# Two moves at the end of each group of a state-space stage: the last fill product ahead of x's transposes, the third chunk's exponents between the result's transposes

## The chip, the core and the metric

The kernel runs on one core of a Trainium2 chip. The core has TensorE (PE in the rows, its weight loads PEld), VectorE (DVE), ScalarE (ACT), GpSimd (POOL) and SyncE (SP, which issues most DMAs). Each engine works its own queue in order. The metric is device time in microseconds, the median of three runs.

## What is computed

Two transformer-like blocks for 512 tokens of width 1024, all in float32. The change touches the first block's state-space branch alone: eight groups of four heads (64 wide, state 128), two scan directions, four chunks of 128 tokens. Of the reference:

```python
xbc = jax.nn.silu(depthwise_conv(xbc, conv_w, conv_b))      # x, b and c of every group
decay = segsum_exp(a_dt)                                    # exp of differences, 128 x 128 per chunk and head
cb = jnp.einsum('bclgn,bcsgn->bcgls', c, b)
y_diag = jnp.einsum('bcgls,bcgrls,bcsgrp->bclgrp', cb, decay, xdt)
states = jnp.einsum('bclgn,bcgrl,bclgrp->bcgrpn', b, decay_states, xdt)
...
y_off = jnp.einsum('bclgn,bcgrpn,bcgrl->bclgrp', c, prev, jnp.exp(a_cs))
...
y = y_fwd + y_bwd + xs * d_skip.astype(jnp.float32).reshape(G, R, 1)
u = y * jax.nn.silu(z.astype(jnp.float32))                  # then a norm per group and the output product
```

## The kernel before, in words

Weights come in units of 1 MB. Each is loaded to a tile `raw`, cast by ACT to its high part `whi` (L140), and DVE makes the low part `wlo` (L141). A product is three products of high and low parts: L286 to L288 with channels on the partitions, L304 to L306 with tokens on them. All of them write the PSUM banks `psg`, of which there are two: a third product starts when the first one's bank has been read.

The loop over the groups runs from about 60 to 505 us. In the loop of group g the state-space work of g is mixed with the products for g + 1. What is issued, and in which order, is written out by hand in the string `GSEQ` (L29 to L31), a list of step names for the groups 0 to 6; group 7 has `LAST_GSEQ`. The names that matter here:

- `z0` to `z3`: the product for z, one for each tile of 128 tokens (L304 to L306). ACT copies each from its bank to `sz` (L630). The first use of a unit also casts the next unit in the stream.
- `f0` to `f7`: the fill, which is the next group's products. In most groups `f4` and `f5` are the two halves of x's first tile of channels, `f6` and `f7` the halves of its second one; for group 4 each of `f4` to `f7` is a whole tile, and `f6`, `f7` are the two of x. After the last half comes `conv_silu` (L587): ACT copies the bank to `cbuf` (L591) and scales it (L592), DVE adds four taps (L594), ACT takes the Silu (L595). L592 is the last reader of the bank.
- `xt0`, `xt1`: four transposes on PE of x's first and second tile (L600), copied by ACT to `xt` (L601). `xt1` is in the next group's loop, behind `z0 w0`.
- `e0` to `e3`: the next group's exponents for a chunk (`exponents`, L677). For each of the two directions one matmul into a bank `pse` (L685, two banks), one Exp on ACT (L687) into `e0` (two buffers) or `e1` (one buffer), one masking on POOL (L688); then one addition on POOL (L692) into `w` (four buffers).
- `w0` to `w3` (L697): cb times the exponents' sum. `cb` (L656). `st0` to `st2` (L667, from `xw`, L664): the states. `y0` to `y3`: the output; ACT ends each with a square and its sum (L724).
- `norm`: an inverse root on POOL (L343), four scalings on ACT (L729).
- `u0`, `u1`: four transposes on PE each (L734) into `pso` and `psy`; ACT makes `ua_h` of each (L337), DVE `ua_l` (L338).
- `rows`: two DMAs per direction for the next group's exponents, issued by POOL (L648, L650).

`GSEQ` isn't the queues' order. The program is built by a framework whose planner walks the traced instructions with the string's order as priority: when, by its own account of durations, an engine is free, it gives it the first instruction by priority whose inputs and buffers are there. So steps that wait are overtaken, and each engine's queue is then fixed. Which activation table ScalarE holds is settled on the finished queue: an `ACT_TABLE_LOAD` stands where Exp follows Silu or the other way round. Copies, scalings and squares go with either table.

Of the kernel before, what the change touches and what calls it, by code (L numbers as in the profile page):

```python
# [26 lines left out]
NF = 8  # L27
LAST_GSEQ = "z0 xt1 st0 w0 z1 st1 w1 z2 w2 st2 z3 w3 silu y0 k0 y1 y2 y3 norm k1 u0 k2 u1 k3"
GSEQ = """  # L29
z0 w0 xt1 st0 z1 w1 z2 z3 st1 silu st2 y0 f0 f1 y1 rows f2 f3 w2 e0 y2 e1 w3 f4 f5 bt y3 norm f6 e2 xt0 f7 u0 u1 cb e3  # L30
"""  # L31
SEQ = """v.0 v.1 v.2 v.3 p0 v.4 n0 v.5 v.6 v.7 c0 G u.0 L0.0 L0.1 L0.2 W0.0 u.1 W0.1 L0.3 p1 W0.2 n1 W0.3 u.2 u.3 f0 c1
L1.0 o.0 o.1 L1.1 W1.0 o.2 L1.2 L1.3 S o.3 p2 P0 W1.1 n2 W1.2 o.4 B0.0 x0 W1.3 o.5 f1 c2 B0.1 o.6 L2.0 L2.1 x1
# [1865 lines left out]
```

## Time and profile before

| what | value |
| --- | --- |
| median of 3 runs | 1914.93 us (1913.95 to 1914.96) |
| the profiled execution, its own time | 1915.58 us |
| its span, first to last instruction | 1913.8 us |
| PE busy | 1846.5 us, 96% |
| ACT, DVE, POOL busy | 937.4, 1142.9, 439.4 us |

The span is what the views below are cut from; 1.8 us of the execution's time lie around it. A row of a timeline gives the start, the length, the engine, the line, the operation, the tiles (out<-in) and how many instructions are merged; in brackets, how long the engine was idle before and what ended that. Rows that follow on one engine overlap a little, so a chain is read from start to start.

### The profile page before, as it was taken

The numbers are of one execution on the slowest core, as the hardware profiler recorded it, in microseconds if no ns is written. First come the engines' busy times: TensorE is split into PE (matmuls) and PEld (weight loads), VectorE is DVE, ScalarE is ACT, GpSimd is POOL, SyncE is SP. The second block draws the span as 40 slices with busy tenths as digits, with TensorE's granted clock in tenths as the row PEclk, the third lists the DMA queues.
The fourth block names the chain that finished last, engine by engine and source line by source line (L and its number), as shares of the span: only waits on it lengthen the run. The fifth ranks groups of instructions, "written<-read, shape, count | busy, mean of one in ns | idle before, by whom it ended". The sixth has DMA issues, their size and how long they took to land. (4 is left out here: it accounts for less than half of the span.)

```text
span 1913.8 us, 24517 instructions
## 1 busy us (share of the span) xinstructions
PE 1846.5 (96%) x9585; PEld 1525.0 (80%) x9585; DVE 1142.9 (60%) x1796; ACT 937.4 (49%) x1511; POOL 439.4 (23%) x498
## 2 busy tenths in 40 slices
PE   8899999999999999998999999989999999999998
PEld 7688888888887777887888888878877768888886
DVE  6767762666456554537233434567667785766768
ACT  6756672766335665345332313345443454444534
POOL 1454441443202321234011201231210330000000
PEclk9999999999999999999999999999999999999999
DMA  5222112221332222333333232322211232324211
GB/s 170 75 68 68 52 62 88 68 68 46 102 93 66 82 79 67 126 119 110 100 98 111 88 110 89 110 74 59 73 45 55 78 132 77 125 85 132 88 44 44
DMA packets 161186, 164.10 MB, mean 86 GB/s; under 512 B 8743, under 2 KB 148718, under 8 KB 161071
## 3 DMA queue, kind: packets, MB, share of 16 engines
q1 hardware_dynamic: 148858, 150.90, 25.0%
q10 hardware_dynamic: 9716, 10.02, 1.7%
q0 software_dynamic: 2496, 1.61, 0.4%
q8 instruction: 75, 1.23, 0.3%
q14 instruction: 41, 0.33, 0.1%
HBM read 158.26 MB, written 4.23 MB: 85 GB/s over the span
## 5 line engine op out<-in xcount | busy, mean ns | idle before, releaser
L141 DVE TENSOR_TENSOR wlo<-raw,whi 128x1024 fp32r<-128x1024 f32 (+3 forms) x253 | 321.4, 1286 | 223.5 <-ACT whi L140 219.3
L286 PE MATMUL psg<-hh,whi 128*128 128x512 f32 (+1 forms) x1016 | 404.2, 398 | 0.8 <-DVE hl L338 0.8
L287 PE MATMUL psg<-hl,whi 128*128 128x512 f32 (+1 forms) x1016 | 401.0, 395 | 0.0
L140 ACT CAST whi<-raw 128x1024 fp32r<-128x1024 f32 (+3 forms) x253 | 254.7, 1028 | 298.4 <-PE psg L287 255.0
L288 PE MATMUL psg<-hh,wlo 128*128 128x512 f32 (+1 forms) x1016 | 399.5, 393 | 0.0
L286 PEld LDWEIGHTS psg<-hh,whi 128*128 128x128 f32 (+1 forms) x1016 | 191.0, 188 | 40.3 <-issue 1.2
L288 PEld LDWEIGHTS psg<-hh,wlo 128*128 128x128 f32 (+1 forms) x1016 | 191.0, 188 | 39.8
L287 PEld LDWEIGHTS psg<-hl,whi 128*128 128x128 f32 (+1 forms) x1016 | 190.9, 188 | 38.2 <-DVE hl L335 0.4
L286 PE MATMUL psg<-ua_h,whi 128*128 128x512 f32 x544 | 216.3, 399 | 0.8 <-DVE xT L1585 0.5
L287 PE MATMUL psg<-ua_l,whi 128*128 128x512 f32 x544 | 213.8, 393 | 0.0
L288 PE MATMUL psg<-ua_h,wlo 128*128 128x512 f32 x544 | 212.7, 391 | 0.0
L304 PE MATMUL psg<-whi,hh 128*128 128x256 f32 x416 | 122.1, 294 | 10.1 <-ACT cacc L592 3.6
L286 PEld LDWEIGHTS psg<-ua_h,whi 128*128 128x128 f32 x544 | 102.0, 188 | 26.0 <-DVE xT L1585 2.4
L305 PE MATMUL psg<-wlo,hh 128*128 128x256 f32 x416 | 119.8, 288 | 1.0 <-DVE wlo L141 1.0
L306 PE MATMUL psg<-whi,hl 128*128 128x256 f32 x416 | 120.2, 289 | 0.0
L287 PEld LDWEIGHTS psg<-ua_l,whi 128*128 128x128 f32 x544 | 102.3, 188 | 21.7 <-issue 1.0
L288 PEld LDWEIGHTS psg<-ua_h,wlo 128*128 128x128 f32 x544 | 102.2, 188 | 20.8
L1187 POOL TENSOR_TENSOR fsq<-relu 128x512 f32<-128x512 f32 x32 | 40.5, 1267 | 243.5 <-ACT relu L1184 228.2
L1009 POOL TENSOR_TENSOR ssq<-ssq,sq 128x512 f32<-128x512 f32 x42 | 66.3, 1578 | 117.2 <-ACT sq L1008 115.9
L141 DVE TENSOR_TENSOR wlo<-quad,whi 128x1024 fp32r<-128x1024 f32 x56 | 66.9, 1222 | 43.0 <-ACT whi L140 43.0
L304 PEld LDWEIGHTS psg<-whi,hh 128*128 128x128 f32 x416 | 80.0, 192 | 15.7 <-ACT sz L630 5.1
L140 ACT CAST whi<-quad 128x1024 fp32r<-128x1024 f32 x56 | 57.0, 1049 | 70.0 <-PE psg L287 32.9
(628 smaller groups left out, 3547.7 us busy)
## 6 DMA issues: line engine op xcount, KB each, us to landing
raw<-in_w_in_dram SPq DMA_DIRECT2D x37, 1024.0 KB
raw<-in_w_mlp_in_dram SPq DMA_DIRECT2D x16, 1024.0 KB
raw<-in_w_mlp_out_dram SPq DMA_DIRECT2D x16, 1024.0 KB
raw<-in_w_ff_dram SPq DMA_DIRECT2D x16, 1024.0 KB
quad<-in_w_ff_dram SPq DMA_DIRECT2D x16, 1024.0 KB
raw<-in_w_in_dram SPq DMA_DIRECT2D x16, 512.0 KB
raw<-in_w_ssd_out_dram SPq DMA_DIRECT2D x8, 1024.0 KB
raw<-in_w_attn_out_dram SPq DMA_DIRECT2D x4, 1024.0 KB
```

The source lines that it names most:

```text
L140: A.copy(self.hi[sl], self.raw[sl])
L141: V.tensor_tensor(out=self.lo[sl], in0=self.raw[sl], in1=self.hi[sl].bitcast(F32), op=ALU.subtract)
L286: T.matmul(o, lhsT=u.hi[:, k, c:e], rhs=xh[k], start=k == 0, stop=False)
L287: T.matmul(o, lhsT=u.hi[:, k, c:e], rhs=xl[k], start=False, stop=False)
L288: T.matmul(o, lhsT=u.lo[:, k, c:e], rhs=xh[k], start=False, stop=k == u.kt - 1)
L304: T.matmul(o, lhsT=xh[k][:, tk], rhs=u.hi[:, k, 0 : u.n], start=k == 0, stop=False)
L305: T.matmul(o, lhsT=xh[k][:, tk], rhs=u.lo[:, k, 0 : u.n], start=False, stop=False)
L306: T.matmul(o, lhsT=xl[k][:, tk], rhs=u.hi[:, k, 0 : u.n], start=False, stop=k == u.kt - 1)
L1009: G.tensor_tensor(out=self.t, in0=self.t, in1=q, op=ALU.add)
L1187: G.tensor_tensor(out=f, in0=r, in1=r, op=ALU.mult)
```

## The change

One line of `GSEQ`. `f7` comes ahead of `xt0`, and `e2` comes behind `u0` and ahead of `u1`. So `e2` is passed by `f7`, `xt0` and `u0`. Nothing is added or removed, and `LAST_GSEQ` stays.

```diff
 GSEQ = """
-z0 w0 xt1 st0 z1 w1 z2 z3 st1 silu st2 y0 f0 f1 y1 rows f2 f3 w2 e0 y2 e1 w3 f4 f5 bt y3 norm f6 e2 xt0 f7 u0 u1 cb e3
+z0 w0 xt1 st0 z1 w1 z2 z3 st1 silu st2 y0 f0 f1 y1 rows f2 f3 w2 e0 y2 e1 w3 f4 f5 bt y3 norm f6 f7 xt0 u0 e2 u1 cb e3
 """
```

## Rows read from the trace of the kernel before

**Rows 1.** The page: its head and the busy time of each engine.
```profile
span 1913.8 us, 24517 instructions
...
PE 1846.5 (96%) x9585; PEld 1525.0 (80%) x9585; DVE 1142.9 (60%) x1796; ACT 937.4 (49%) x1511; POOL 439.4 (23%) x498
```

**Rows 2.** Busy time in stretches: the change-over from group 2 to group 3, then one whole period. Columns: stretch, its length, busy us (and instructions) of each engine, granted PE clock, DMA share, GB/s.
```profile
206.00:229.00 23.00, 20.12 (x135) 17.57 (x133) 15.81 (x21) 18.56 (x31) 14.36 (x20) 1.00 0.22 64
212.00:264.00 52.00, 49.24 (x284) 42.29 (x284) 36.16 (x51) 33.64 (x56) 24.67 (x35) 1.00 0.20 63
```

**Rows 3.** PE in order of time, 206 to 229 us: `e2`, `cb`, and every start that came after a wait.
```profile
206.90 0.62 PE L685 MATMUL pse<-rh,lh 128*128 128x512 f32 x2
...
210.07 1.05 PE L656 MATMUL psc<-cT,bT 128*128 128x128 f32 x8
...
213.01 0.66 PE L600 MATMUL pst<-ident,cacc 128*128 128x128 f32 x4 [1.19 <-ACT cacc L595]
...
218.07 0.39 PE L304 MATMUL psg<-whi,hh 128*128 128x256 f32 x1 [0.58 <-ACT cacc L592]
...
222.35 0.39 PE L304 MATMUL psg<-whi,hh 128*128 128x256 f32 x1 [0.39 <-ACT sz L630]
...
226.17 0.66 PE L600 MATMUL pst<-ident,cacc 128*128 128x128 f32 x4 [0.20 <-ACT cacc L595]
...
228.48 0.70 PE L667 MATMUL pso<-xw,bt 128*128 128x256 f32 x2 [0.46 <-DVE xw L664]
```

**Rows 4.** ACT in order of time, 208 to 226 us.
```profile
208.83 0.19 ACT L724 ACTIVATION_READ_ACCUMULATOR xd<-sz 128x1 f32 x1
209.04 1.28 ACT L687 ACT_TABLE_LOAD   x1
210.33 0.60 ACT L687 ACTIVATE e<-pse 128x512 f32<-128x512 f32 x1
210.94 1.28 ACT L595 ACT_TABLE_LOAD   x1
212.24 0.72 ACT L595 ACTIVATE cacc<-cacc,pv 128x512 f32<-128x512 f32 x1
212.87 1.69 ACT L729 ACTIVATE sz<-sz,ssg 128x256 f32<-128x256 f32 x4
214.58 1.28 ACT L687 ACT_TABLE_LOAD   x1
215.87 0.60 ACT L687 ACTIVATE e<-pse 128x512 f32<-128x512 f32 x1
...
216.83 0.60 ACT L591 COPY cbuf<-psg 128x512 f32<-128x512 f32 x1
217.31 0.71 ACT L592 ACTIVATE cacc<-psg,pv 128x512 f32<-128x512 f32 x1
217.89 0.71 ACT L337 ACTIVATE ua_h<-pso,pv 128x512 fp32r<-128x512 f32 x1
...
219.03 1.13 ACT L687 ACTIVATE e<-pse 128x512 f32<-128x512 f32 x2
219.98 2.05 ACT L140 CAST whi<-raw 128x1024 fp32r<-128x1024 f32 x2
221.86 0.71 ACT L630 COPY sz<-psg 128x256 f32<-128x256 f32 x2
...
223.58 1.28 ACT L595 ACT_TABLE_LOAD   x1
225.39 0.72 ACT L595 ACTIVATE cacc<-cacc,pv 128x512 f32<-128x512 f32 x1 [0.53 <-DVE cacc L594]
```

**Rows 5.** DVE in the same stretch: the last tap for x's first tile, the first and last tap for its second.
```profile
209.13 0.75 DVE L594 SCALAR_TENSOR_TENSOR cacc<-cbuf,pv,cacc 128x512 f32<-128x512 f32 x1
...
218.05 1.67 DVE L594 SCALAR_TENSOR_TENSOR cacc<-cbuf,pv,cacc 128x512 f32<-128x512 f32 x1 [5.60 <-ACT cacc L592]
...
224.25 1.11 DVE L594 SCALAR_TENSOR_TENSOR cacc<-cbuf,pv,cacc 128x512 f32<-128x512 f32 x1
```

**Rows 6.** POOL in the same stretch: the norm's root, `e2`'s addition.
```profile
209.30 1.48 POOL L343 TENSOR_TENSOR ssg<-ssg,mhalf 128x4 f32<-128x4 f32 x1 [2.76 <-DVE ssg L342]
...
217.87 1.30 POOL L692 TENSOR_TENSOR w<-e,e 128x512 f32<-128x512 f32 x1
```

**Rows 7.** ACT from 355 to 369 us, the change-over from group 4 to 5.
```profile
355.50 1.28 ACT L687 ACT_TABLE_LOAD   x1
356.79 1.09 ACT L687 ACTIVATE e<-pse 128x512 f32<-128x512 f32 x2
357.90 1.28 ACT L595 ACT_TABLE_LOAD   x1
359.19 0.72 ACT L595 ACTIVATE cacc<-cacc,pv 128x512 f32<-128x512 f32 x1
...
368.85 0.36 ACT L630 COPY sz<-psg 128x256 f32<-128x256 f32 x1
```

**Rows 8.** PE's waits in three other change-overs: the longest of group 0 to 1, of group 4 to 5, and the last one before the loop of group 7.
```profile
114.07 0.39 PE L304 MATMUL psg<-whi,hh 128*128 128x256 f32 x1 [0.73 <-ACT cacc L592]
...
359.97 0.66 PE L600 MATMUL pst<-ident,cacc 128*128 128x128 f32 x4 [1.11 <-ACT cacc L595]
...
472.91 0.39 PE L304 MATMUL psg<-whi,hh 128*128 128x256 f32 x1 [1.15 <-ACT sz L630]
```

## The prediction

> **What bounds the kernel now.** I read the page first: of a span of 1913.8 us PE is busy for 1846.5, so whatever order is chosen, PE's work stays and only its waits can go [rows 1]. Then the busy times by stretch: in a whole period of the group loop PE is idle for 52.00 - 49.24 = 2.76 us, and almost all of that lies in the 23 us around the change of groups, where PE is idle for 2.88 us [rows 2]. Then PE in order of time, which shows the five waits of one change-over: 1.19 for the Silu of x's first tile, 0.58 for the bank that x's second tile leaves (L592), 0.39 for z0's copy, 0.20 for the Silu of x's second tile, 0.46 for the states' operand, 2.82 together [rows 3]. Then ACT over the same stretch, since it ends four of the five: from the table load at 209.04 to z0's copy at 221.86 it is never idle, and three loads stand in that stretch, Exp, Silu, Exp [rows 4]. So in the change-over ACT sets PE's pace. There are seven change-overs: four like this one (after groups 1, 2, 3 and 5), and those after groups 0, 4 and 6. If every wait went, at most 7 x 2.8 = 20 us could be gained, 1%.
>
> **What the change moves on PE.** f7 already runs ahead of x's transposes: cb follows it at 210.07, the transposes start at 213.01 [rows 3]. So the first move changes little by itself; what moves is e2. Its two matmuls at 206.90, a row of 0.62 us, land behind f7 and still ahead of cb, because x's first tile isn't ready then. What f7 gains in place e2 loses: nothing in sum. No instruction and no DMA is added.
>
> **What it moves on ACT, step by step, in a steady change-over.**
> - The square ends at 209.02. Before, the Exp load and e2's first Exp came next; now e2's matmuls are not done, and the Silu of x's first tile waits for DVE's last tap, 209.13 + 0.75 = 209.88 [rows 5]. ACT idles for 0.9 us. The table is still Silu's, so this Silu runs at 209.9 and not at 212.24: the 1.19 wait goes.
> - The copy of x's second bank goes into the gap before the norm's root, which POOL ends at 210.78 [rows 6]. Four scalings (212.87 to 214.58, 1.7) bring it to 212.7. Then L592 starts, at 212.7 and not at 217.31: the 0.58 wait goes. It takes 0.58 from start to start (217.31 to 217.89), to 213.3 [rows 4].
> - Then, by the same rows' starts, xt's copy (0.48, as the copy of a bank from 216.83 to 217.31), ua_h of u0 (0.57, half of 217.89 to 219.03), the Exp load (1.29), e2's two Exps (219.03 to 219.98, 0.95), ua_h of u1 (0.57) and e3's first Exp (half of 0.95): 217.6. The next group's casts follow (219.98 to 221.86, 1.88): 219.5 [rows 4].
> - e3's second Exp can't follow its first: its buffer e1 is single, and e2's addition on POOL must end first. Before, that took from 216.47, where the second Exp ended, to 217.87 + 1.30 = 219.17, so 2.7 us [rows 4, 6]. From e2's end at 216.6 it is 219.3. Meanwhile the second tile's taps, which DVE starts at 213.3 and not at 218.05, are done; before, four taps with other work between took from 218.05 to 225.36 [rows 5], but the two halves of the cast and POOL's traffic are not in the way now, and I take 4 to 5 us, so 217.3 to 218.3. The order is fixed at build; if the planner's durations are like the rows', x's Silu, which stands ahead of e3 in the list, is taken first, with a Silu load before it and an Exp load behind it: 1.29 + 0.63 (212.24 to 212.87) + 1.29 + 0.48 = 3.7, and z0's copy starts at 219.5 + 3.7 = 223.2, that is 1.4 us later than 221.86 [rows 4].
>
> So two of three loads are not saved, they are moved, and a 0.63 us Silu that stood behind z0's copy at 225.39 now stands ahead of it. PE reaches the third product for z sooner and waits there for z0's copy: **+1.4**. In that wait it does the four transposes of x's second tile, which came later before: -0.42 (the row is 0.66 long and its end overlaps what follows; between 0.3 and 0.66). The last two waits, 0.20 and 0.46, go, because that tile is ready earlier: -0.66. Sum of a steady change-over: 1.4 - 0.42 - 0.66 = **+0.3 us**, four times +1.2.
>
> After group 6 the same +1.4 - 0.42, but there the row shows no late wait to save (its last wait, 1.15, is the one for z's copy [rows 8]): +1.0. After group 4, where f6 and f7 are whole tiles, the two loads at 355.50 and 357.90 go from ahead of x's Silu and with them the wait of 1.11 [rows 7, 8]; e2's Exps (1.09) and one more switch back (1.29) go in ahead of z0's copy at 368.85: -1.11 + 1.09 + 1.29 - 0.66 = +0.6, of which I take +0.5, as part of the wait may remain. After group 0 I have only a wait of 0.73 for L592 [rows 8]: between -0.7 (it goes) and +1.4 (as steady, nothing saved), and take 0, since both effects act there. Sum: 1.2 + 1.0 + 0.5 + 0 = **+2.7 us**.
>
> What is late elsewhere: e2's masking and addition move from 217.87 to some 218 on POOL, ahead of nothing urgent; the DMA issues of `rows` on POOL stand behind e3's matmuls as before. I cost them at nothing; their cover is the two matmuls of the next e0, and without it PE would lose the 0.62 us of such a row in each change-over, within the bounds.
>
> The price of a table switch carries the rivals. From load to Exp it is 210.33 - 209.04 = 1.29 us, and ACT starts the load 0.02 us after the accumulator read ends [rows 4]. The Trainium skill, "ScalarE: Activation LUTs", section What ACT_TABLE_LOAD costs, gives 1283 ns for the load, which agrees, and some 1380 ns more for a drain, 2.66 us for a switch. The rows have no room for that drain; by the page each switch saved would weigh twice as much, and the second rival below would come to some -10 us.
>
> The sum stands against the profiled execution, 1915.58 us (span 1913.8 and 1.8 around it): 1918.3. That execution is 0.65 above the median of 1914.93, so on the median's footing **1917.6**.
>
> **The rivals.**
> 1. *Z's copies come first* (0.15). If the taps of x's second tile last until z0's copy is issued, as before, where that Silu came 3.5 us after it [rows 4], and e3 isn't held up, only one load is left in the stretch: z0's copy moves by 1.4 - 2 x 1.29 - 0.63 = -1.8, the late waits go too, -2.5 in all, inside the 2.82. Four times -2.5, after group 6 -1.8, after group 4 -1.1, after group 0 -0.7: -13.6, so 1901.3. For it: Silu came late before. Against it: its taps start 4.7 us earlier. The same page's Rules for kernel authors speak for this one: do all of one table set before switching. By that rule alone the change pays.
> 2. *One switch fewer* (0.20). e3's second Exp is ready before x's second Silu and goes ahead of it. Then the switch back is not needed before z0's copy: -1.29 each, so 4 x -1.0, -0.3, -0.8 and 0: -5.1, so 1909.8. It decides on some 1 us between POOL's addition and DVE's taps.
> 3. *Slower* (0.17). The copy of x's second tile stands behind z0's on ACT, and the states' operands behind the casts' low halves on DVE. If xt1 is so late that its transposes and the states fill nothing, the credits of 0.42 and 0.66 fall away: +1.4 in five change-overs, +1.2 after group 4, +1.4 after group 0, +9.6, so 1924.5. It decides where PE reaches the third z product before xt1's Silu has ended.
> 4. *It changes nothing* (0.10): f7 was ahead already, and e2's Exps keep their place between others; 1914.9.
>
> **How the numbers follow.** My forecast has 0.38. Its own range is 1914 to 1921 (group 0's two ends and half a microsecond for each of the others). The range of 1905 to 1924 leaves out the first rival and the upper part of the third, some 2 in 10. A measurement of this kernel can tell about 0.2%, 3.8 us, from no change. Faster by more: all of the first rival, most of the second, little else: 0.33. Slower by more: the third and a third of the forecast: 0.27. Between: 0.40. Cases of both signs hold the chance nearly evenly, so the likeliest is a difference too small to see.
>
> **What would show it.** Right: in the profile after, x's first transposes without a wait behind cb; PE's wait for z0's copy grown from 0.4 to about 2 to 3 us; on ACT, in each change-over, a Silu load between e3's two Exps, ahead of z0's copy. Wrong: z0's copy earlier than before against f7's end, or only one load between the square and z0's copy (rival 1), or e3's Exps side by side (rival 2); transposes of x's second tile still behind the third z product (rival 3). As many loads as before in the group loop would bear the forecast out.

## The result, and the profile after

The changed kernel takes **1941.11 us** (median; 1939.44 to 1943.00) against 1914.95 before: a ratio of 1.0132, interval 1.0116 to 1.0148. It is slower by 26 us, outside the forecast's range and beyond the rival that ended on the slow side. The profiled execution took 1942.12 us. The head of its page, against [rows 1]:

```profile
span 1940.4 us, 24489 instructions
...
PE 1856.3 (96%) x9585; PEld 1534.7 (79%) x9585; DVE 1139.0 (59%) x1796; ACT 935.4 (48%) x1509; POOL 438.2 (23%) x498
```

PE runs the same 9585 matmuls and is busy 9.8 us longer; ACT has two instructions fewer. So PE waits longer, and its work takes longer. The two need not add up to the loss, since slower work can fill a wait; the part on why the prediction was wrong comes back to that. The whole group stage shows both. Columns as in [rows 2]; first the kernel before, then the changed one.

```profile
60.00:501.00 441.00, 415.74 (x2315) 352.50 (x2315) 281.43 (x401) 273.37 (x439) 192.96 (x268) 0.99 0.21 64
```

```profile
60.00:528.00 468.00, 427.07 (x2327) 363.88 (x2326) 278.76 (x403) 271.70 (x437) 191.84 (x268) 0.96 0.21 61
```

The stage's last transposes of the result end at 501.0 us before and at 527.5 after, so all 26.5 us are lost here. Of the 27 between the two stretches, 15.7 are idle time of PE (25.3 to 40.9) and 11.3 are busy time, at a granted clock of 0.96 instead of 0.99. The waits of PE in the stage, grouped by what ended them (total us, times, longest); first before, then after:

```profile
PE pst L600 <- ACT cacc L595: 8.0, 11, 1.2
PE psg L304 <- ACT cacc L592: 3.6, 6, 0.7
...
PE pse L685 <- DMA lh<-gld: 0.2, 1, 0.2
```

```profile
PE pst L600 <- ACT cacc L595: 16.6, 9, 3.9
PE pse L685 <- DMA lh<-gld: 9.9, 9, 2.1
```

The wait that the forecast took away has doubled (8.0 to 16.6), and one that it costed at nothing, of the next group's `e0` for its rows, has appeared (9.9). Only the wait for the bank, L592, is gone as forecast. PE in the change-over from group 2 to 3, against [rows 3]:

```profile
222.74 0.66 PE L600 MATMUL pst<-ident,cacc 128*128 128x128 f32 x4 [2.58 <-ACT cacc L595]
...
224.60 1.06 PE L656 MATMUL psc<-cT,bT 128*128 128x128 f32 x8
...
231.15 0.66 PE L600 MATMUL pst<-ident,cacc 128*128 128x128 f32 x4
...
233.63 0.47 PE L685 MATMUL pse<-rh,lh 128*128 128x512 f32 x1 [0.99 <-DMA lh<-gld]
234.91 0.64 PE L685 MATMUL pse<-rh,lh 128*128 128x512 f32 x1 [0.81 <-ACT whi L140]
235.35 0.44 PE L304 MATMUL psg<-whi,hh 128*128 128x256 f32 x1
235.59 0.42 PE L305 MATMUL psg<-wlo,hh 128*128 128x256 f32 x1
235.80 0.41 PE L306 MATMUL psg<-whi,hl 128*128 128x256 f32 x1
...
240.13 0.28 PE L304 MATMUL psg<-whi,hh 128*128 128x256 f32 x1
240.25 0.28 PE L305 MATMUL psg<-wlo,hh 128*128 128x256 f32 x1
```

x's first transposes stand directly behind f7; cb, which before filled 0.9 us of that gap, comes 1.9 us behind them. And from 235.35 on a z matmul follows the one ahead of it after 0.24 and 0.21 us, at 240.25 after 0.12: from 235 to 236 the granted clock is 0.52, so PE runs there at the lower of its two levels (1.2 GHz). After the longer wait, from 222.74 to 230.00, it is 1.00. ACT in the same stretch, against [rows 4]:

```profile
219.19 0.19 ACT L724 ACTIVATION_READ_ACCUMULATOR xd<-sz 128x1 f32 x1
221.16 0.91 ACT L729 ACTIVATE sz<-sz,ssg 128x256 f32<-128x256 f32 x2 [1.79 <-POOL ssg L343]
221.98 0.71 ACT L595 ACTIVATE cacc<-cacc,pv 128x512 f32<-128x512 f32 x1
222.59 0.90 ACT L729 ACTIVATE sz<-sz,ssg 128x256 f32<-128x256 f32 x2
...
223.85 0.68 ACT L592 ACTIVATE cacc<-psg,pv 128x512 f32<-128x512 f32 x1
...
225.61 1.28 ACT L687 ACT_TABLE_LOAD   x1
...
229.07 1.28 ACT L595 ACT_TABLE_LOAD   x1
230.37 0.73 ACT L595 ACTIVATE cacc<-cacc,pv 128x512 f32<-128x512 f32 x1
231.11 1.28 ACT L687 ACT_TABLE_LOAD   x1
232.41 0.60 ACT L687 ACTIVATE e<-pse 128x512 f32<-128x512 f32 x1
232.90 1.98 ACT L140 CAST whi<-raw 128x1024 fp32r<-128x1024 f32 x2
234.78 0.38 ACT L630 COPY sz<-psg 128x256 f32<-128x256 f32 x1
```

The order from `e3`'s first Exp on is the forecast's. Ahead of it is the surprise: two of the norm's scalings stand before the Silu of x's first tile. They need the root, and the Silu's own operand is there earlier. DVE's last tap and POOL, against [rows 5, 6]:

```profile
219.48 0.74 DVE L594 SCALAR_TENSOR_TENSOR cacc<-cbuf,pv,cacc 128x512 f32<-128x512 f32 x1
```

```profile
219.66 1.47 POOL L343 TENSOR_TENSOR ssg<-ssg,mhalf 128x4 f32<-128x4 f32 x1 [2.77 <-DVE ssg L342]
...
230.20 1.29 POOL L692 TENSOR_TENSOR w<-e,e 128x512 f32<-128x512 f32 x1
231.43 0.57 POOL L650 DMA_DIRECT2D lh<-gld  x1
```

The taps end at 220.22, the root at 221.13; the Silu could have started 1.8 us earlier. On POOL a `rows` DMA is issued behind `e2`'s addition, at 231.43, for a matmul that PE reaches at 232.6. PE waits there, ahead of the third product for z, which then follows without a wait for z0's copy. Group 0 to 1, first before, then after, ACT from the last square's read to z0's copy:

```profile
107.93 0.19 ACT L724 ACTIVATION_READ_ACCUMULATOR xd<-sz 128x1 f32 x1
108.13 1.28 ACT L687 ACT_TABLE_LOAD   x1
...
117.89 0.69 ACT L630 COPY sz<-psg 128x256 f32<-128x256 f32 x2
```

```profile
108.84 0.19 ACT L724 ACTIVATION_READ_ACCUMULATOR xd<-sz 128x1 f32 x1
...
114.23 1.28 ACT L687 ACT_TABLE_LOAD   x1
...
118.62 1.28 ACT L595 ACT_TABLE_LOAD   x1
...
120.66 1.28 ACT L687 ACT_TABLE_LOAD   x1
...
123.38 0.38 ACT L630 COPY sz<-psg 128x256 f32<-128x256 f32 x1
```

**One measure for all kernels.** I cut each period at two starts on ACT: the last square's read and z0's copy. Between them lies "the chain", from the copy to the next period's last read "the rest". In us for the change-overs after groups 0, 1, 2, 3, 4, 5, 6:

| | chain | sum | rest | sum |
| --- | --- | --- | --- | --- |
| before | 9.96, 13.03, 13.03, 13.03, 19.20, 13.03, 13.03 | 94.3 | 38.66, 39.26, 39.22, 75.53, 38.29, 39.23, 24.11 | 294.3 |
| after | 14.54, 16.30, 15.59, 15.59, 20.43, 16.09, 15.59 | 114.1 | 40.39, 39.12, 39.43, 75.70, 40.60, 39.11, 26.37 | 300.7 |

Three quarters of the loss, 19.8 us, is in the chain, the work of ACT around the change of groups; 6.4 are in the rest, nearly all of it after groups 0, 4 and 6 (1.7, 2.3 and 2.3). In the four steady rests, after groups 1, 2, 3 and 5, it is 0.1 in sum.

### The profile page after: what moved, and what is told of

Its sections match the earlier page's. It is cut to its first block, busy times and chain, and to the rows that moved or that the text cites. A ratio compares the mean times of both kernels' runs of the same rounds, so it can differ in the third digit from the quotient of the medians.

```text
span 1940.4 us, 24489 instructions
## 1 busy us (share of the span) xinstructions
PE 1856.3 (96%) x9585; PEld 1534.7 (79%) x9585; DVE 1139.0 (59%) x1796; ACT 935.4 (48%) x1509; POOL 438.2 (23%) x498
## 5 line engine op out<-in xcount | busy, mean ns | idle before, releaser
L141 DVE TENSOR_TENSOR wlo<-raw,whi 128x1024 fp32r<-128x1024 f32 (+3 forms) x253 | 325.8, 1305 | 238.0 <-ACT whi L140 233.7
```

The lines of the kernel that those rows point to most:

```text
L141: V.tensor_tensor(out=self.lo[sl], in0=self.raw[sl], in1=self.hi[sl].bitcast(F32), op=ALU.subtract)
```

## The experiments

Each edit is to the changed kernel unless it says otherwise; a list is the end of `GSEQ`, and a line `...` in a diff stands for lines left out. Letters of theories are those of the text quoted with them. A ratio, with its interval, is to the kernel before as timed along with that experiment (medians of 1914.11 to 1917.02 us), so ratios compare better than medians.

**Which of the two moves?** One kernel makes the first move alone, one the second.

```diff
-... norm f6 f7 xt0 u0 e2 u1 cb e3
+... norm f6 e2 f7 xt0 u0 u1 cb e3     # e1_f7_alone
+... norm f6 xt0 f7 u0 e2 u1 cb e3     # e2_e2_alone
```

> Only the first move: f7 ahead of xt0, e2 still between f6 and f7. Theory A (missing filler): the loss comes from e2's leaving its place, because with e2's Exps out of ScalarE's way the planner takes x's first tile for ready when f7 ends and puts its transposes directly behind f7; here e2 stays, cb, e3 and z stand between f7 and the transposes as in the kernel before, so the time is that of before, 1915 within 4 us, with PE's wait at x's first transposes about 1.2 us. Theory R (the first move costs by itself, f7 taking the bank earlier): about half of the loss or more, 1928 to 1941.

> Only the second move: e2 between u0 and u1, f7 still listed behind xt0. Theory A: the transposes stand directly behind f7 in PE's queue although the list has them ahead of it, so the time is that of after, 1936 to 1945, with waits of about 2.6 us at the first transposes. Theory R (first move): close to before, 1912 to 1920.

The first alone: 1919.89 us, ratio 1.0021 [1.0004, 1.0038]. The second alone: 1942.8, ratio 1.0154 [1.0115, 1.0194]. The second move brings the loss; the first alone costs some 0.2%. With the first alone the chain stays 13.03 in steady change-overs; only group 0's grows, 9.96 to 12.06, with a second table load in it. Ten table loads more stand in its ACT queue, nine of them in the rests, whose sum is 295.0 against 294.3: there they cost next to nothing.

**The scalings ahead of the Silu.** The four scalings are queued behind it.

```diff
-    A.activation(dst, dst, AF.Silu, bias=pcol(R_CB + ch))
+    conv_silu.last = A.activation(dst, dst, AF.Silu, bias=pcol(R_CB + ch))
...
-    A.activation(self.sz[:, c, :], self.sz[:, c, :], AF.Copy, scale=self.ss[:, c : c + 1])
+    with tc.issue_after(conv_silu.last.ins): A.activation(self.sz[:, c, :], ...)
```

> The kernel after, with the four scalings of the norm queued on ScalarE behind the Silu of x's first tile. Theory A1 (the Silu stands behind two scalings that wait for POOL's root; that is what PE waits for): the wait at the first transposes falls from 2.6 to about 0.8 us, some 1.5 us gained in each of 5 to 6 change-overs, 1930 to 1934. Theory A2 (there is nothing between f7 and the transposes of x and of the result, and the result's wait for the scalings in turn): the wait moves on to L734, gain under 0.5 us per change-over, 1937 to 1943.

1934.5 us, ratio 1.0105 [1.0073, 1.0137]: 7 us less than with the change by the medians, 5 by the ratios, and the two intervals overlap, so the times alone do not prove the gain. The rows show the step that theory A1 named. PE's wait in the steady change-over falls from 2.58 to 0.91, but the chain only from 15.59 to 14.97, since ACT still waits, 0.89 for the taps and 0.18 for the root. The waits for `lh` grow from 9.9 to 13.7 in sum.

**The late rows for e0.** Its two matmuls are queued behind the last z product.

```diff
-    T.matmul(pe, lhsT=lh[d][:, sl], rhs=rh[d], start=True, stop=True)
+    with ExitStack() as o: behind is not None and o.enter_context(tc.issue_after(behind.ins)); T.matmul(pe, ...)
...
```

> The kernel after, with the two matmuls of the next group's e0 queued on PE behind the last product for z, so that they no longer stand ahead of the third z product and wait there for the DMA of lh. Theory B (late DMAs are the loss): the 9.9 us of waits for lh in the group loop go, and the time falls by 7 to 10 us, to 1931 to 1934. Theory A with ScalarE as the bound: the third z product waits for z0's copy instead, and the time stays, 1937 to 1943.

The waits for `lh` are gone, and the time is worse, outside both ranges: 1958.24, ratio 1.022 [1.0189, 1.0252]. PE now waits 14.6 us (7 times) for z's copy, which comes no sooner (the sum of the chains is 116.9). So the late DMAs stood in front of a wait that ends later still; they are not the cause of the long chain. The time is not their price: the rest grows too, from 300.7 to 316.2 in sum, and why is not shown.

**x's second Silu out of the chain.** As the third experiment, and that Silu a step of its own, `sx`, queued behind z0's copy (in the last group's list too).

```diff
-z0 w0 xt1 st0 z1 ...
+z0 sx w0 xt1 st0 z1 ...
...
```

> e3_silu_first, and the Silu of x's second tile traced as a step of its own and queued on ScalarE behind the first z copy, as it stood in the kernel before. Then one table load (Exp, ahead of e2) stands ahead of z0's copy in place of three, and e3's two Exps are side by side. Theory S (what is left of the loss is ScalarE's queue ahead of z0's copy): z0's copy comes 3 x 0.6 to 1.3 us earlier in each of six change-overs, 1934.5 - 10 to - 15: 1919 to 1925. Theory B (what is left are late DMAs for the next e0): 1931 to 1936.

1927.05, ratio 1.0059 [1.0042, 1.0075]; less gained than expected. One table load is left in the chain instead of three, but the chain only falls from 14.97 to 13.65: where two loads and the Silu stood (3.2 us), ACT now waits, 0.96 for the matmul of `e3` and 0.94 for `e2`'s addition on POOL. The rest is 40.65, with PE busy for 39.25 of it at a full clock, against 38.12 before: more of PE's work falls into it. The Silu that is put off is hardly waited for, 1.1 us once in all; the 12.2 us that PE waits for Silus are for those that keep their place, in a steady change-over 2.29 for the one of x's first tile. The Trainium skill, "ScalarE: Activation LUTs", section Rules for kernel authors, says to do all of one table set before switching. Here two switches fewer in each chain do not bring back the time of before, since other waits stand where the loads stood and the rest is longer.

**The change of groups laid out anew.** The end of the list is moved into the next group's loop, behind z0, and in the second kernel `e2` and `e3` behind z1 and z3 (`p0`, `p1` are the last group's u0, u1; `LAST_GSEQ` is changed to match).

```diff
-z0 w0 xt1 st0 z1 w1 z2 z3 ... norm f6 f7 xt0 u0 e2 u1 cb e3
+z0 xt0 p0 e2 p1 cb e3 w0 xt1 st0 z1 w1 z2 z3 ... norm f6 f7      # e6_z0_between
+z0 xt0 p0 p1 cb w0 xt1 st0 z1 w1 e2 z2 z3 e3 ... norm f6 f7      # e7_e2e3_late
...
```

> The kernel after, with the end of the list (xt0 u0 e2 u1 cb e3) moved into the next group's loop, behind z0: a product for z of 2.9 us stands between f7 and x's transposes on PE. Theory A (missing filler): the 2.6 us wait there is gone in every change-over; if nothing takes its place, 1941 - 6 x 2.6 - clock = 1920 to 1927. Theory S (ScalarE's queue ahead of z0's copy bounds the change-over anyway): the wait comes back as one for L630 or L592, 1933 to 1942.

> As e6_z0_between, and e2 and e3 listed behind z1 and z3, so that no Exp and no table load stand on ScalarE between the square of y3 and the copies of z. Theory S: both waits go (transposes, z copy), and this is faster than the kernel before, 1898 to 1910. Rival: the exponents are late for w2 and w3 and the rows' DMAs late for the next e0, and the time is 1912 to 1925.

1933.14 (ratio 1.0097 [1.0081, 1.0112]) and 1931.81 (1.0086 [1.0069, 1.0103]); the first lies at the low end of theory S's range, though with another wait than it names; the second is 22 us above theory S's range and 7 above the rival's. The chain is short in both, 10.11 and 8.20, and the rest of a steady period long, 41.9 to 48.7. In the first, PE waits 3.2 for x's transposes but 16.5 for a bank that an Exp has to free; in the second, 24.1 for the Silus, more of it for the second tile (3.17 against 1.10 in a steady change-over). Here a short chain does not pay, because what is put off is needed in the rest.

**PE kept busy in the wait.** Twelve constant matmuls ahead of x's first transposes.

```diff
-    pt = bank("t")
+    pt = bank("t"); [T.matmul(pt[:, 0:P], lhsT=ones, rhs=ones, start=True, stop=True) for _ in range(busy)]
...
```

> The kernel after with twelve matmuls of constants (128x128, float32) ahead of the transposes of x's first tile, about 2.5 us of PE work whose result is overwritten: in each change-over PE is busy where it waited. Theory C (part of the loss is TensorE's clock, which falls behind PE's waits): the half-clock stretches at the transposes go, the granted clock of the span rises from 0.985 to 0.99 or more, and the time falls by 3 to 8 us although nothing useful was added, 1933 to 1938. Rival (the clock doesn't follow these waits): 1941 to 1948, the clock as before.

1959.88, ratio 1.0234 [1.0217, 1.0251], at a mean clock of 0.989 against 0.985. Both ranges are missed. The planner rearranged the queues for it (the waits for the states' operand grow from 6.3 to 16.6, and 16.3 for the Exps are new), so it says nothing on what the clock costs.

**Does it matter where PE waits?** cb as a filler ahead of the transposes, ACT's order in a steady change-over unchanged; and f7 first with `e2` directly behind it.

```diff
-... norm f6 f7 xt0 u0 e2 u1 cb e3
+... norm f6 f7 cb xt0 u0 e2 u1 e3     # e9_cb_ahead
+... norm f6 f7 e2 xt0 u0 u1 cb e3     # e10_e2_behind_f7
```

> The changed list with cb moved from behind u1 to between f7 and xt0; PE then has cb's eight matmuls (0.9 us) between f7 and x's first transposes, and ScalarE's queue is as in the changed kernel. Theory A (PE's wait for the Silu of x's first tile is itself the loss, because nothing stands between f7 and the transposes): that wait falls from 2.58 to about 1.7 in a steady change-over, 9 times 0.9 less in sum, and the time falls by 6 to 8 us, to 1933 to 1936. Rival B (ScalarE's chain up to z0's copy is the bound, PE's filler only says where PE waits): the wait for the transposes falls by as much, the waits of the next e0's matmuls or for z0's copy grow by as much, and the time stays within 3 us of 1941.

> f7 ahead of e2 as in the changed kernel, but e2 ahead of xt0 and u0, and not between u0 and u1. By the order built, e2's matmuls run between f7 and x's transposes (0.5 us), cb behind u1, and on ScalarE the scalings of the norm stand as in the changed kernel, two of them ahead of the Silu of x's first tile; e2's two Exps stand ahead of xt's copy and ua_h. Theory A (the loss comes from e2's Exp no longer standing ahead of the Silu, which puts two scalings ahead of it, and from the missing filler): about as slow as the changed kernel, 1935 to 1943, PE's wait for the first transposes about 2 us. Rival C (the loss comes from e2 standing between u0 and u1, the second move as such): 1915 to 1922, as with the first move alone.

The first: 1942.36, ratio 1.0127 [1.0105, 1.0148], no gain. PE in the same change-over:

```profile
217.45 1.05 PE L656 MATMUL psc<-cT,bT 128*128 128x128 f32 x8
220.23 0.66 PE L600 MATMUL pst<-ident,cacc 128*128 128x128 f32 x4 [1.72 <-ACT cacc L595]
...
225.05 0.50 PE L685 MATMUL pse<-rh,lh 128*128 128x512 f32 x1 [0.90 <-ACT e L687]
```

The wait falls by 0.86 and comes back 5 us later as 0.90; the chain is 15.60 (216.68 to 232.28), as after. Rival B holds: ACT's chain sets the pace, and PE's order only says where it waits. The second kernel: 1933.23, ratio 1.0078 [1.0056, 1.0101], between the two theories. Its chain is 15.61 too. Its profiled execution took 1940.44 us at a mean clock of 0.985, like the changed kernel's; the three others, at 0.990 to 0.992, took 1932.49 to 1933.57. So `e2`'s passing of the transposes and u0 is not needed for the long chain: that it stands behind f7 is enough. By the ratios some 15 of the 25 us come with it; where the other 10 lie is not shown, since the one execution that was profiled is the longest of the four.

**A version meant to beat both.** `e2` directly behind `e1`, cb as filler, the scalings behind the Silu; in the second kernel `e3` ahead of x's transposes as well.

```diff
-... w2 e0 y2 e1 w3 f4 f5 bt y3 norm f6 f7 xt0 u0 e2 u1 cb e3
+... w2 e0 y2 e1 e2 w3 f4 f5 bt y3 norm f6 f7 cb xt0 u0 u1 e3     # e11_e2_early
+... w2 e0 y2 e1 e2 w3 f4 f5 bt y3 norm f6 f7 cb e3 xt0 u0 u1     # e12_e2_early_e3_first
```

> A version meant to beat both: e2 directly behind e1, some 10 us ahead of the change-over, where its Exps share the table load of e1's; f7 and cb ahead of x's first transposes; the four scalings queued behind the Silu of x's first tile. By the order built, ScalarE has from the last square to z0's copy Silu, 4 scalings, copies, both ua_h, one Exp load, e3's two Exps, two casts, a Silu load, x's second Silu: two loads where before had three. Theory A (what counts is how soon the Silu of x's first tile ends after f7, with a filler on PE, and how many loads stand ahead of z0's copy): wait for the transposes below 0.5, wait for the second tile's bank gone, wait for z0's copy about 1, against 2.8 in all before: 1905 to 1912. Rival: e2's Exps and maskings in the stretch of y2 delay y2's or w3's work by as much; 1914 to 1920.

> As the last one, but e3 ahead of x's first transposes, behind cb: its two matmuls are a further filler on PE (0.5 us), and its Exps stand ahead of xt's copy and ua_h; the Silu load and x's second Silu stand ahead of the two casts and z0's copy. Theory A: transposes without a wait; z0's copy comes as late as in the last one, since the same work stands ahead of it: within 4 us of the last one, 1904 to 1912. Rival: xt's copy and ua_h 2.3 us later hold the banks of the transposes and of u0 and u1, and the second Silu, now ahead of the casts, waits for its taps: 1914 to 1922.

1923.04 (ratio 1.003 [1.0016, 1.0043]) and 1919.43 (1.001 [0.9999, 1.002]): neither beats the kernel before. Theory A is missed in both; the first is beyond its rival too, the second inside its rival's range. The steady chain is 12.61 in both (but 15.33 after group 5 in the first), 0.42 under before's. The group stage of the second:

```profile
60.00:506.00 446.00, 423.02 (x2320) 357.13 (x2319) 280.57 (x403) 272.57 (x438) 197.29 (x268) 0.97 0.21 64
```

PE idles 23.0 us, 2.3 less than before, but is busy for 7.3 more, at a clock of 0.97 instead of 0.99. It looks as if the clock had taken the gain, but the chains speak against that: the one after group 1 is 12.62 at a granted clock of 0.86, with PE idle for 1.16, and those after groups 2 and 3 are 12.61 at 1.00, with PE idle for 2.4. The loss is in one change-over. From one last read to the next the second kernel needs 53.23 us after group 0 against 48.62 before, with three table loads in front of z0's copy where there was one, and the other six periods are 0.7 shorter in sum. What makes the clock fall here and not in the kernel before I have not shown.

**The root.** The largest new piece of the chain is the 1.79 us in which ACT waits for the norm's root. In both kernels the root is replaced by a multiplication on POOL, with every queue in the same order; the results then lack the root.

```diff
-    inv_rms(self.ss, self.ss, 256, NT)
+    V.tensor_scalar(out=self.ss, in0=self.ss, scalar1=1.0 / 256, scalar2=EPS, op0=ALU.mult, op1=ALU.add)
+    G.tensor_tensor(out=self.ss, in0=self.ss, in1=mhalf[:, 0:NT], op=ALU.mult)
```

> The changed kernel with the norm's inverse root replaced by a multiplication of the same four columns on POOL (the root itself is left out); every queue keeps its order. Theory B (the period follows ScalarE's chain from the last square to z0's copy, 15.59 us against 13.03 before): the scalings start some 1.3 us earlier, the chain shortens by 1.2 to 1.4 us, PE's wait for the Silu of x's first tile falls from 2.58 to about 1.3, and the time falls by 7 x 1.0 to 1.4, 7 to 10 us, to 1931 to 1935. Rival D (the late DMA for the next e0's matmuls or the states' operand sets the period): the wait for the transposes falls as much, those two grow by as much, and the time stays within 3 us of 1941.

> The same replacement in the kernel before, every queue in unchanged order. Theory B: there the root ends at 210.78 and the scalings start at 212.87, behind the Exp, two table loads and the Silu; nothing in a steady change-over can move, and the time stays within 2 us of 1915. If it falls by more than 4 us, the root is on the path of the kernel before as well and the pair says nothing of the change.

In the changed kernel: 1933.95, ratio 1.0102 [1.0084, 1.0119]; in the kernel before: 1912.82, 0.9987 [0.9976, 0.9999]. So the root was worth 7 us in the one (5.7 by the ratios), inside theory B's range, and 1 to 2.5 in the other. Each is little more than its interval; the rows are clearer than the times. POOL, then ACT, in the changed kernel's variant:

```profile
215.96 0.63 POOL L727 TENSOR_TENSOR ssg<-ssg,mhalf 128x4 f32<-128x4 f32 x1 [2.77 <-DVE ssg L727]
```

```profile
215.49 0.19 ACT L724 ACTIVATION_READ_ACCUMULATOR xd<-sz 128x1 f32 x1
216.63 0.91 ACT L729 ACTIVATE sz<-sz,ssg 128x256 f32<-128x256 f32 x2 [0.95 <-POOL ssg L727]
...
230.25 0.37 ACT L630 COPY sz<-psg 128x256 f32<-128x256 f32 x1
```

The multiplication takes 0.63, the root took 1.47: 0.84 less. The idle time falls by 0.84 (1.79 to 0.95) and the chain by 0.84 (15.59 to 14.75); the period from one last read to the next goes from 55.02 to 54.11. The sum of the chains falls by 6.9 (114.1 to 107.2), and the rest stays (300.7 and 301.1). In the kernel before, the steady chain is 13.03 with and without the root, and only those after groups 0 and 4 are shorter (9.13 and 18.34). In its steady change-over the Exp, two table loads and the Silu stand between square and scalings and cover the root. So these rows show one thing that the second move took away, this cover. What the whole cover is worth is not shown: 0.84 of the 1.79 us bring back about a quarter of the loss.

## Why the prediction was wrong

**The first bound was right.** ACT sets the pace of the change-over. The order of `e3`'s Exps, x's second Silu, its two loads, casts and z0's copy came as forecast, the three loads of a steady change-over too, and the wait for L592 is gone. z0's copy is later, as forecast, by 2.56 and not by 1.4. The wait for it, named as a sign, does not show under that name in a steady change-over: the matmuls of the next `e0` stand in front of the third product for z and wait there instead, 0.99 and 0.81 us.

**The first step that failed**: "the table is still Silu's, so this Silu runs at 209.9 and not at 212.24: the 1.19 wait goes". I let the Silu go first because its taps end before the root, 209.88 against 210.78. The planner gave ACT two scalings first; why is not on record, since its own durations are not. The Silu started 2.79 us after the square's read and not 1.07, and x's transposes had nothing between them and f7, for the planner put them there too, not behind cb. The wait became 2.58. The scalings queued behind the Silu bring back 5 to 7 of the 26 us, a root shorter by 0.84 us some 6 to 7, the first of them not clear of noise.

**The term for ACT** in a steady change-over was +1.4 (13.03 to 14.4) and measured +2.56. Of the missing 1.2, 0.8 is there at L592 already (4.66 us after the read, forecast 3.87), behind the root. The 2.56 are nearly all in two pieces: idling for the root, 1.79 where before ACT was never idle, and the second Silu, 0.63, the one that I had counted.

**The second step that failed: the credits of 1.08.** They were to shorten the rest, and the steady rest is as long as before. After group 2, before, then after:

```profile
221.86:261.09 39.23, 38.12 (x208) 32.45 (x208) 30.28 (x44) 20.96 (x37) 16.45 (x23) 1.00 0.23 73
```

```profile
234.78:274.21 39.43, 38.98 (x204) 33.39 (x205) 27.48 (x40) 20.28 (x35) 15.63 (x21) 0.96 0.23 72
```

PE idles 0.45 instead of 1.11, but it is busy for 38.98, where 38.12 less the four transposes (0.42) would be 37.70. Read alone, this says that the credits came and that the clock, 0.96, took them. The rest after group 3 says otherwise; before, then after:

```profile
274.12:349.65 75.53, 74.31 (x367) 62.47 (x368) 33.26 (x45) 30.72 (x49) 17.08 (x21) 1.00 0.28 84
```

```profile
289.80:365.50 75.70, 74.04 (x364) 62.16 (x365) 30.50 (x41) 30.07 (x48) 16.29 (x19) 1.00 0.29 84
```

Here the clock is full in both, and the rest is no shorter: PE idles 1.66 instead of 1.22. The states' matmuls in the changed kernel, after group 2 and after group 3, then DVE after group 3:

```profile
238.59 1.47 PE L667 MATMUL pso<-xw,bt 128*128 128x256 f32 x4 [0.24 <-DVE xw L664]
```

```profile
293.63 1.47 PE L667 MATMUL pso<-xw,bt 128*128 128x256 f32 x4 [1.59 <-DVE xw L664]
```

```profile
288.99 3.84 DVE L141 TENSOR_TENSOR wlo<-raw,whi 128x1024 fp32r<-128x1024 f32 x2 [1.75 <-ACT whi L140]
292.75 1.60 DVE L664 TENSOR_TENSOR xw<-xt,tok 128x256 f32<-128x256 f32 x2
```

Both times these matmuls start 3.8 us after z0's copy. DVE makes their operand behind the low halves of both casts, so it does not come sooner because x's second tile is ready sooner. The wait of 0.20 is gone, but the one of 0.46 that was to go is 1.59 at the full clock; at half clock PE's slower work fills most of it. So the steady period after group 2 grew by 2.56 in the chain and 0.21 in the rest, 2.77 and not 0.3. The clock was not in my sum at all. In this rest it has no price that shows: with cb ahead of the transposes and with the short root the same rest is 39.44 and 39.35 at a full clock. What it costs in the whole stage is open.

**Group 0**, taken at nothing between -0.7 and +1.4, measured +6.3: chain 9.96 to 14.54, rest +1.7. In front of z0's copy there are three loads where there was one. I had read only its longest wait on PE [rows 8] and not its ACT queue; had I counted its loads as I did in [rows 4], the second Silu with its two loads, 3.2 us, would have been in the bound. Here the Silu of x's first tile does run ahead of the scalings, as forecast, so this loss is not the one of the first step. The granted clock in this rest is 0.93. **Group 4**, +0.5 in the forecast: +1.2 in the chain and +2.3 in the rest, where PE waits 1.5 for `lh` and 1.2 for the states' operand instead of 0.5. **Group 6**, +1.0: +2.6 and +2.3; there z's copy is waited for 2.6 instead of 1.2, and PE runs at 0.94 where it ran at 1.00 (with `e2` directly behind f7 this rest is 26.33 at a full clock, so the clock need not be the cause). The four steady ones, forecast +1.2 together, gave 3.1, 2.8, 2.7 and 2.9, 11.6 in sum. In all 6.3 + 11.6 + 3.5 + 4.8 = 26.2.

**Costed at nothing**: the rows of the next `e0`. The waits for them are real, 9.9 us, but the experiments on e0 and on cb say that they stand in place of others. **The rivals**: the first two needed a chain that gets shorter. The third ended on the right side, and half of its mechanism came: the states' operand stands behind the casts' low halves, and the credits fell away. Its condition did not: x's second transposes ran at 231.15, inside the wait. Its size left out the root and group 0. The switch price was right: where the operand is there, a load is followed by its Exp or Silu after 1.30 us, and no drain shows.

## What to carry to other kernels

Before moving an instruction out of a stretch, ask what it covers: an Exp with two table loads between a square and the scalings looked like cost, and it hid a slow root that nobody waited for. Before counting slower work as lost time, look for a stretch with the same work at full clock: here it was as long, with a wait in place of the slow work. Where a planner sets the order, two instructions that become ready within a microsecond of each other are two cases, each with its own price. And read each change-over's own queue: the first of seven carried a quarter of the loss.

## What the runs showed of the hardware

- PE's clock: at the lower of its two levels a 128x256 matmul followed the last after 0.21 us instead of 0.12. In the group stage the kernel before has 6.8 us of it, the changed one 37.5 and the second early-`e2` version 23.9, though the last one waits less than the kernel before. It did not simply follow the waits: in the changed kernel PE waited 2.58, 0.99 and 0.81 us in the change-over after group 2 and 2.60, 1.11 and 0.55 in the next, and the clock fell behind the first set only. It also differs between executions of one kernel: 1940.44 us at 0.985 and 1932.49 at 0.991.
- Half clock does not always cost time. The changed kernel's rest after group 2 is 39.43 us at 0.96, and in two variants 39.35 and 39.44 at 1.00. With `e2` directly behind f7 it is 41.06 at 0.92, and in that kernel's rests after groups 1 and 5 it is 39.05 and 39.09 at 1.00.
- POOL needs 1.47 us for the root of 128x4 elements in a steady change-over (1.02 to 1.95 over all eight groups), 0.63 for their multiplication, and about 0.1 for a memset of 128x2.
